# A hybrid decoder layer on one core: substitution's loads put ahead of its copies, heads' sums in two rounded passes, output projection's loads of rows and weights put amid tiles of x

## The chip, the core and the metric

The kernel runs on one core of one Trainium2 chip. The metric is device time in microseconds (us), the median of several runs; lower is better. Engines are named as the profile names them: PE multiplies matrices and transposes through a multiplication with the identity, PEld loads its weights, DVE and ACT work element by element, POOL does the small rest, and SP issues all DMAs of this kernel, in order, on one queue.

## The reference

One layer: a linear recurrence (RWKV-7) of 8 heads and forgetting attention of 8 heads share one input projection; their outputs share one output projection; a gated MLP with a short convolution follows. Everything is float32, 1024 tokens, 1024 channels.

```python
h = rmsnorm(x, norm_mix_w)
p = h @ w_in                                   # 1024 x 3848
y_rwkv = rwkv7_group(p[..., :1792], ...)       # state S: [64, 64] a head
y_fox  = fox_group(p[..., 1792:], ...)         # causal softmax with decay
x = x + concat([y_rwkv, y_fox]) @ w_out
h = rmsnorm(x, norm_ffn_w)
x = x + conv_glu_ffn(h, w_up, conv_w, conv_b, w_down)   # 2816 wide, twice
return rmsnorm(x, norm_final_w)

# in rwkv7_group, two sums over the 64 channels of a head:
kk = heads(k * k_k)
kk = kk * rsqrt(maximum(sum(kk * kk, axis=-1, keepdims=True), 1e-24))
bonus = sum(r_h * k_h * r_k, axis=-1, keepdims=True) * v_h
```

## The kernel before

**Precision.** A big product is made of three PE passes in the type `fp32r`: both operands are split into `hi` (a rounded copy, made by ACT as a CAST) and `lo` (the rest, source minus `hi`, made by DVE as a TENSOR_TENSOR), and `hi*hi + hi*lo + lo*hi` is added up in PSUM. Small products and transposes take plain float32 operands; the trace then holds two MATMUL records for a product of 512 columns.

**What sets the order.** No engine chooses its work at run time. The program is a set of generators ("streams"); each yields one instruction, or a list that must stay together, or a condition to wait for. A planner (`Streams`, line 56 on; all instructions are issued in its line 193, so every row of the profile says L193) keeps a time per engine from a cost table, takes the instruction that could start first, and breaks ties by `RANK` (line 35; the lower number goes first). The result is a fixed order for each engine. A moved rule therefore changes the order of nearly everything behind it.

**Stages, in the profile's names.**
- Input projection: `r` (14 column tiles of the recurrence, 672 matmuls with 512 columns) and then `t<-whi/wlo,hhi/hlo` (attention's columns, 1536 matmuls with 256 or 264 columns). Both are called *dense* below. They have PSUM banks and buffers of their own and fill PE wherever the other streams wait. `late` may start when all 2208 are done.
- Recurrence: names with `u_`, 8 *units* (4 pairs of heads, two halves of the tokens each), one stream for each step: `front` (decays; `ss` is the heads' sum of squares, `beta` comes from it), `gram`, `slots` (`bps` is the heads' sum for the bonus), `taken_out`, `inverse`, `placed`, `solve`, `chain` (the state's steps), `output`.
- The stream `inverse` inverts 32x32 triangles by substitution on POOL. `taken_out` writes the triangles to `dsub` in DRAM; `inverse` loads them four times, each time for 32 partitions of the tile `ml`, lets ACT copy a quarter of each into `mw`, runs 60 POOL instructions and stores `mw` to `dinv`; `placed` loads that into `tbd`, which `solve` needs.
- Attention (once all 8 units are out and the pools are handed over): `s` (scores), `t<-ident,pr` (transposes of the weights), `po` (products), `tt` (tails); `tq` turns queries and keys.
- Output projection, `op`: a first pass over 4 of 8 row tiles of `w_out` for all 8 token tiles (96 matmuls; allowed between attention's steps, since dense is then done), the sum put aside in `sp_x`, and a second pass for the rest (288). `plan` (line 1329) is the order in which the stream `late_loads` issues their loads and `late_splits` makes `hi` and `lo` of them: kinds `wo` (a tile of `w_out`), `y` (a row tile of the inputs that went to DRAM), `xh` (half a token tile of x, which the first pass adds to), `x`. The raw loads share four buffers (tag `f2`) with the input projection's evictions; the split weights share four `whi` and four `wlo` buffers, which come free when the last token tile has used them.
- MLP: `hT`, `A` to `F` (up), `dx` and `dy` (down).

The order of POOL's and SP's other work around the change comes from the same planner.

Of the kernel before, what the change touches and what calls it, by code (L numbers as in the profile page):

```python
# [32 lines left out]
INF = float("inf")  # L33

RANK = dict(rates=4, loads=2, params=4, fills=3, normed=4, turned=4, weights=3, splits=3, dense=9, evac=0, forget=8,
            chain=1, solve=2, inverse=7, taken_out=0, placed=6, front=3, gram=0, slots=4, output=5, stages=0, late_splits=8,
            late_loads=3, late=9, products=5, load_pairs=6, values=3, scores=0, soft=4, turned_back=2, tail=7,
            added=3, parts=1, summed=4, turned_again=4, combined=2, up_loads=6, sums=2.5, up_splits=2.5, down_loads=7,
            down_splits=2.5, token_loads=5, conv=9, combined_2=3,
# [235 lines left out]
def hymba_layer(tc, x, norm_mix_w, w_in, rwkv_mu, rwkv_w0, rwkv_w2, rwkv_a0, rwkv_a2, rwkv_g2, rwkv_k_k, rwkv_k_a,  # L275
# [8 lines left out]
    with whole:  # L284
# [5 lines left out]
        ident = cst.tile([P, P], F32, name="ident")  # L290
        make_identity(nc, ident)
        Q.given.update([ident.name] + [f"in_{n}" for n in _INS])
        oblk = cst.tile([P, P], F32, name="oblk")
        ones = cst.tile([P, P], F32, name="ones")
        mhalf = cst.tile([P, 16], F32, name="mhalf")
        prm = cst.tile([P, C_END], F32, name="prm")
        cvw = cst.tile([P, 3, 2 * NFF], F32, name="cvw")
        Q.do(V.memset(mhalf, -0.5), V.memset(oblk, 0.0), V.memset(oblk[0:64, 0:64], 1.0),
             V.memset(oblk[64:128, 64:128], 1.0), V.memset(ones, 1.0),)


        sp_r = {(j, p, h): dr.tile([P, HALF], F32, name=f"sp_{j}_{p}_{h}") for j in "rkv" for p in range(4)
# [441 lines left out]
        def names(i):  # L744
# [11 lines left out]

            return p, hf, u, tl, rp, col

        def front(i):
            p, hf, u, tl, rp, col = names(i)  # L760
            q = units[i]
# [9 lines left out]

            sq = tl("t2", "sq", [P, HALF], 6)
            yield S.activation(sq, kt_, AF.Square, scale=col(C_KK))
            pt = yield from rp("ss")
            yield PE.matmul(pt, lhsT=oblk, rhs=sq, start=True, stop=True)
            beta = tl("t2", "beta", [P, HALF], 6)
            yield V.tensor_scalar(beta, pt, scalar1=1e-24, scalar2=0.0, op0=ALU.max, op1=ALU.add)
            Q.release(pt)
# [79 lines left out]
        def slots(i):  # L858

            p, hf, u, tl, rp, col = names(i)  # L860
            q = units[i]
            yield has(i, "gram")
            kb = q["kb"]
            yield has(i - 2, "chain")
            kbt = tl("kbt", "kbt", [P, 8, P], 2)
            for nq in range(2):
                pt = yield from rp(f"kbt{nq}")
                for i4 in range(4):
                    n = nq * 4 + i4
                    m, o = divmod(n, 2)  # L870
                    yield PE.transpose(pt[:, i4 * P:(i4 + 1) * P],
                                       kb[:, m, 2 * o:2 * o + 2, :].rearrange("p a c -> p (a c)"), ident)
                yield S.copy(kbt[:, nq * 4:nq * 4 + 4, :].rearrange("p n c -> p (n c)"), pt)
                Q.release(pt)
            q["kbt"] = kbt
            yield lambda: ("r", 8 + p, hf) in done
            yield has(i - 2, "output")
            bv = tl("bv", "bv", [P, HALF], 2)
            yield SP.dma_start(bv, sp_r["v", p, hf])
            vu = tl("vu", "vu", [P, 8, P], 2)  # L880
            vu4 = vu.rearrange("p (m o) c -> p m o c", o=2)
            pt = yield from rp("vt")
            for m in range(4):
                yield PE.transpose(pt[:, m * P:(m + 1) * P], bv[:, m * P:(m + 1) * P], ident)
            yield S.copy(vu4[64:128, :, 0, :], pt[0:64].rearrange("p (m c) -> p m c", c=P))
            yield S.copy(vu4[0:64, :, 1, :], pt[64:128].rearrange("p (m c) -> p m c", c=P))
            Q.release(pt)
            q["vu"] = vu
            pt = yield from rp("bps")
            yield PE.matmul(pt, lhsT=oblk, rhs=q["rk"], start=True, stop=True)  # L890
            q["bonus"] = True
            yield V.tensor_tensor(bv, bv, pt, op=ALU.mult)
            Q.release(pt)
            q["bv"] = bv
# [14 lines left out]
        def inverse(i):  # L909
# [7 lines left out]
            ml = tl("ml", "ml", [P, 32, 32], 1)  # L917
            mw = tl("mw", "mw", [P, 8, 32], 1)
            tmp = tl("mtmp", "mtmp", [P, 72], 1)
            mwf = mw.rearrange("p a t -> p (a t)")  # L920
            for g in range(4):
                gs = slice(g * 32, g * 32 + 32)
                yield SP.dma_start(ml[gs], dsub.rearrange("q o b s t -> (q o b) s t"))
                yield S.copy(mw[gs], ml[gs, g::4, :])
            for s in range(1, 31):
                w, n = 31 - s, (s + 3) // 4
                tv = tmp[:, 0:n * w].rearrange("p (s t) -> p s t", t=w)
# [2 lines left out]
                yield G.tensor_tensor(mw[:, 0:n, s + 1:32], mw[:, 0:n, s + 1:32], tv, op=ALU.add)  # L930
            for g in range(4):
                yield G.memset(mwf[g * 32:g * 32 + 32, g::36], 1.0)
            for g in range(4):
                yield SP.dma_start(dinv.rearrange("q o b s t -> (q o b) s t")[:, g::4, :],
                                   mw[g * 32:g * 32 + 32])
            q["dinv"] = dinv

        def placed(i):
            q = units[i]
# [389 lines left out]
        def plan():  # L1329
            for kt in range(4):  # L1330
                yield "wo", (0, kt), w_out[0, kt * P:(kt + 1) * P, 0:HALF]
            for kt in range(7):
                for hf in (1, 0):
                    yield "y", (hf, kt), y_v[:, kt, half(hf)]
                if kt == 3:
                    for tb in TOKENS:
                        yield "xh", tb, x8[tb][:, 0:HALF]
            for j, k0, tbs in ((0, 4, ()), (1, 0, TOKENS[0:4]), (1, 4, TOKENS[4:])):
                for kt in range(k0, k0 + 4):
                    yield "wo", (j, kt), w_out[0, kt * P:(kt + 1) * P, half(j)]  # L1340
                for tb in tbs:
                    yield "x", (0, tb), sp_x[tb]
# [644 lines left out]
```

## Time and profile before

| | |
|---|---|
| time, median of 3 runs | 1462.68 us (1462.61 to 1465.28) |
| the profiled execution | 1458.29 us, its span 1456.5 us |
| busy in the span: PE, PEld, DVE, ACT, POOL | 1404.3, 1159.0, 1061.2, 712.8, 300.6 us |
| mean granted PE clock | 0.996 |
| 50 to 552.4 us: recurrence and dense | PE busy 492.47 of 502.40 us |
| 552.4 to 722.8 us: attention, rest of dense, first `op` | PE busy 158.11 of 170.40 us |
| 722.8 to 799.6 us: rest of `op` | PE busy 72.82 of 76.80 us |
| from 799.6 us: MLP | PE busy 644.71 of 656.90 us |

A matmul's duration in a row is longer than its share of PE, since matmuls overlap: what it costs is the step from its start to the next one's start. "Idle" is time with no matmul under way. Rows of the timeline give start, duration, engine, line, operation, `out<-in`, shapes, count, and in brackets the idle time before with what ended it.

### The profile page before, as it was taken

The page shows a single profiled execution, that of the slowest core. Times are in us where ns is not written, and L with a number is a line of the kernel's source. Part 1 is how long each engine was busy: PE and PEld are TensorE (multiplying, and loading weights), DVE is VectorE, ACT ScalarE, POOL GpSimd, SP SyncE. Part 2 cuts the span into 40 slices and gives each one's busy share as a digit, 9 for nine tenths or more (in the row PEclk, how much of TensorE's full clock was granted, in tenths as well). Part 3 has the DMA queues.
Part 4 walks back from the last instruction along what each step waited for, and adds up shares of the span by engine and source line. Part 5 has one row for each costly group of instructions (what it writes and reads, how often), then busy time and mean ns, then how long its engine had stood idle before and what let it go on. Part 6 is the DMA issues. An engine that isn't in the chain of part 4 may idle for free.

```text
span 1456.5 us, 23416 instructions
## 1 busy us (share of the span) xinstructions
PE 1404.3 (96%) x8105; PEld 1159.0 (80%) x8105; DVE 1061.2 (73%) x2036; ACT 712.8 (49%) x1339; POOL 300.6 (21%) x772
## 2 busy tenths in 40 slices
PE   6999999999999999989999989999999999999997
PEld 4777877889999998667678868888888888888886
DVE  5387567877775546787546898988887776896575
ACT  6643344445343336777533654455544544444453
POOL 3006553365465212433301000000000000000011
PEclk9999999999999999999999999999999999999999
DMA  5544333433422335474271134555652225864342
GB/s 178 195 120 136 97 95 111 123 102 100 113 68 78 87 104 154 136 213 132 90 267 65 62 113 156 190 188 195 202 167 80 73 86 187 305 199 139 95 152 87
DMA packets 198099, 198.12 MB, mean 136 GB/s; under 512 B 39979, under 2 KB 135773, under 8 KB 197981
## 3 DMA queue, kind: packets, MB, share of 16 engines
q1 hardware_dynamic: 197981, 196.63, 43.5%
q8 instruction: 64, 1.05, 0.3%
q14 instruction: 54, 0.44, 0.1%
HBM read 139.13 MB, written 57.44 MB: 135 GB/s over the span
## 4 chain that ended last, share of the span: by engine, by line
PE 77%; DVE 9%; DMA 6%; issue 3%; ACT 3%; SPq 1%; POOL 1%; DVEq 0%; POOLq 0%; ACTq 0%
PE B L193 16%; PE t L193 9%; PE r L193 8%; PE C L193 8%; PE dx L193 8%; PE dy L193 6%; PE op L193 4%; PE A L193 4%; PE u_uy L193 1%; DMA qraw<-sp_q 1%; PE s L193 1%; SPq L193 1%; PE po L193 1%; DMA x<-in_x 1%; DMA raw<-in_w_out 1%
## 5 line engine op out<-in xcount | busy, mean ns | idle before, releaser
L193 PE MATMUL t<-whi,hhi 128*128 128x256 f32 (+1 forms) x512 | 149.5, 292 | 1.2 <-ACT whi L193 0.8
L193 PE MATMUL t<-whi,hlo 128*128 128x256 f32 (+1 forms) x512 | 149.8, 293 | 0.0
L193 PE MATMUL t<-wlo,hhi 128*128 128x256 f32 (+1 forms) x512 | 149.1, 291 | 0.3 <-DVE wlo L193 0.3
L193 POOL TENSOR_SCALAR fms<-fms 128x1 f32<-128x1 f32 x8 | 2.4, 295 | 609.4 <-ACT fsq L193 609.1
L193 POOL TENSOR_TENSOR u_mtmp<-u_mw,u_ml 128x60 f32<-128x60 f32 (+10 forms) x240 | 79.1, 330 | 147.7 <-ACT u_mw L193 129.6
L193 ACT CAST dwhiP<-dP 128x512 fp32r<-128x512 f32 x77 | 47.7, 620 | 107.6 <-PE dy L193 48.4
L193 PEld LDWEIGHTS t<-whi,hhi 128*128 128x128 f32 x512 | 96.6, 189 | 3.6 <-ACT whi L193 1.0
L193 PEld LDWEIGHTS t<-wlo,hhi 128*128 128x128 f32 x512 | 96.6, 189 | 2.0 <-issue 1.0
L193 PEld LDWEIGHTS t<-whi,hlo 128*128 128x128 f32 x512 | 96.7, 189 | 1.9 <-issue 1.4
L193 PE MATMUL r<-hhi,whi 128*128 128x512 f32 x224 | 92.1, 411 | 0.9 <-DVE edge L193 0.6
L193 PE MATMUL r<-hlo,whi 128*128 128x512 f32 x224 | 92.7, 414 | 0.0
L193 PE MATMUL r<-hhi,wlo 128*128 128x512 f32 x224 | 91.7, 410 | 0.5 <-DVE wlo L193 0.5
L193 DVE TENSOR_TENSOR dwloP<-dP,dwhiP 128x512 fp32r<-128x512 f32 x77 | 53.1, 689 | 51.2 <-ACT dwhiP L193 50.8
L193 POOL TENSOR_TENSOR u_mw<-u_mw,u_mtmp 128x60 f32<-128x60 f32 (+10 forms) x240 | 83.9, 350 | 18.6
L193 DVE SCALAR_TENSOR_TENSOR yv<-uv,cvw,yv 128x1023 f32<-128x1023 f32 (+1 forms) x44 | 56.3, 1280 | 38.9 <-ACT yv L193 38.8
L193 PE MATMUL dx<-dwhiP,glP 128*128 128x512 f32 x176 | 69.4, 394 | 0.0
L193 PE MATMUL dx<-dwhiP,ghP 128*128 128x512 f32 x176 | 69.4, 394 | 0.0
L193 PE MATMUL dx<-dwloP,ghP 128*128 128x512 f32 x176 | 69.0, 392 | 0.0
L193 DVE SCALAR_TENSOR_TENSOR yg<-ug,cvw,yg 128x1023 f32<-128x1023 f32 (+1 forms) x44 | 56.4, 1282 | 7.6 <-ACT yg L193 6.7
L193 ACT CAST whi<-wraw 128x512 fp32r<-128x512 f32 (+1 forms) x60 | 37.0, 619 | 38.8 <-PE r L193 17.6
L193 ACT ACTIVATE pr<-pr,mx 128x1024 f32<-128x1024 f32 (+7 forms) x64 | 49.6, 779 | 9.3 <-DVE mx L193 9.1
L193 DVE TENSOR_TENSOR glP<-gb,ghP 128x512 fp32r<-128x512 f32 x77 | 52.7, 684 | 0.7 <-ACT ghP L193 0.6
(953 smaller groups left out, 4123.4 us busy)
## 6 DMA issues: line engine op xcount, KB each, us to landing
a<-in_ffn_w_up SPq DMA_DIRECT2D x88, 256.0 KB
wraw<-in_w_in SPq DMA_DIRECT2D x108, 128.0 KB
sp_gv<-yg SPq DMA_DIRECT2D x22, 512.0 KB
dB<-in_ffn_w_down SPq DMA_DIRECT2D x44, 256.0 KB
sp_T<-dB SPq DMA_DIRECT2D x44, 256.0 KB
gb<-sp_gv SPq DMA_DIRECT2D x44, 256.0 KB
dP<-sp_T SPq DMA_DIRECT2D x44, 256.0 KB
dP<-in_ffn_w_down SPq DMA_DIRECT2D x33, 256.0 KB
```

The costliest lines, as they stand in the source:

```text
L193: fn(*args, **kw)
```

## The change

It has three parts.

1. **Heads' sums.** `oblk` (the block matrix of ones) becomes `fp32r`, made from `ones`. `ss` and `bps` (8 of each) go through a new stream piece `head_sums`: ACT makes a rounded copy `hi`, DVE the rest `lo`, both in `f2` buffers, and PE adds two `fp32r` passes in one bank.
2. **Substitution.** `inverse` issues its four loads of `ml` first and its four copies to `mw` after them. The POOL part becomes a stream of its own, `substituted`, with the old rank 7; `inverse` itself (loads, copies, stores) and `placed` get rank 0.
3. **Output projection's loads.** `plan` puts all eight `y` items of the recurrence's rows first, then `xh` of four token tiles, then the `y` items of row tiles 4 and 5, `xh` of two, the `wo` tiles 4 and 5, `xh` of the last two, `y` of row tile 6, and `wo` 6 and 7. Before, all eight `xh` came ahead of `y` 4 to 6 and all four `wo`.

```diff
-RANK = dict(... solve=2, inverse=7, taken_out=0, placed=6, ...
+RANK = dict(... solve=2, inverse=0, taken_out=0, substituted=7, placed=0, ...
...
-        oblk = cst.tile([P, P], F32, name="oblk")
+        oblk = cst.tile([P, P], F32R, name="oblk")
...
+        def head_sums(name, src):
+
+            hi = yield from Q.take(fp, [P, HALF], F32R, "f2", f"{name}_hi", 4)
+            yield S.copy(hi, src)
+            lo = yield from Q.take(fp, [P, HALF], F32R, "f2", f"{name}_lo", 4)
+            yield V.tensor_tensor(lo, src, hi, op=ALU.subtract)
+            pt = yield from bank("rp", name, 3)
+            yield [PE.matmul(pt, lhsT=oblk, rhs=hi, start=True, stop=False),
+                   PE.matmul(pt, lhsT=oblk, rhs=lo, start=False, stop=True)]
+            Q.release(hi)
+            Q.release(lo)
+            return pt
...
-            pt = yield from rp("ss")
-            yield PE.matmul(pt, lhsT=oblk, rhs=sq, start=True, stop=True)
+            pt = yield from head_sums(f"{u}_ss", sq)
...
-            pt = yield from rp("bps")
-            yield PE.matmul(pt, lhsT=oblk, rhs=q["rk"], start=True, stop=True)
+            pt = yield from head_sums(f"{u}_bps", q["rk"])
...
+            quarters = [slice(g * 32, g * 32 + 32) for g in range(4)]
+            for gs in quarters:
+                yield SP.dma_start(ml[gs], dsub.rearrange("q o b s t -> (q o b) s t"))
+            for g, gs in enumerate(quarters):
+                yield S.copy(mw[gs], ml[gs, g::4, :])
+            Q.spawn("substituted", substituted(q, ml, mw, tmp))
+            yield has(i, "substituted")
...
-            for g in range(4):
-                gs = slice(g * 32, g * 32 + 32)
-                yield SP.dma_start(ml[gs], dsub.rearrange("q o b s t -> (q o b) s t"))
-                yield S.copy(mw[gs], ml[gs, g::4, :])
...
-            for kt in range(7):
+            def ys(kt):
                 for hf in (1, 0):
                     yield "y", (hf, kt), y_v[:, kt, half(hf)]
-                if kt == 3:
-                    for tb in TOKENS:
-                        yield "xh", tb, x8[tb][:, 0:HALF]
-            for j, k0, tbs in ((0, 4, ()), (1, 0, TOKENS[0:4]), (1, 4, TOKENS[4:])):
-                for kt in range(k0, k0 + 4):
+
+            def xhs_of(tbs):
+                for tb in tbs:
+                    yield "xh", tb, x8[tb][:, 0:HALF]
+
+
+            for kt in range(4):
+                yield from ys(kt)
+            yield from xhs_of(TOKENS[0:4])
+            yield from ys(4)
+            yield from ys(5)
+            yield from xhs_of(TOKENS[4:6])
+            for kt in (4, 5):
+                yield "wo", (0, kt), w_out[0, kt * P:(kt + 1) * P, 0:HALF]
+            yield from xhs_of(TOKENS[6:8])
+            yield from ys(6)
+            for j, k0, tbs in ((0, 6, ()), (1, 0, TOKENS[0:4]), (1, 4, TOKENS[4:])):
+                for kt in range(k0, (k0 + 4) & ~3):
```

**What stands where now.** In instructions, PE has 7241 instead of 7225, ACT 1254 instead of 1237, DVE 2053 instead of 2038, POOL 777 as before, SP 963 instead of 960 DMAs. From about the middle of the second `op` pass on, all five engines have the same order as before.

First place: SP, where unit 0's triangles go out to `dsub` and come back in `ml` (`sp_v`, `sp_k` and `sp_r` are rows of the projection that wait in DRAM, `u_bv`, `u_r`, `u_xs`, `u_k` and `u_ta` the units' loads of such rows, `wraw` weights of the input projection). Before:

```order
L193 DMA u_dsub<-u_ga 32x8x32 x4
L193 DMA u_bv<-sp_v_0_93 128x512
L193 DMA u_ml<-u_dsub 32x1024
L193 DMA sp_v_1_94<-pm_1_1149 128x512
L193 DMA u_ml<-u_dsub 32x1024
L193 DMA u_r<-sp_r_1_78 128x512
L193 DMA u_ml<-u_dsub 32x1024 x2
L193 DMA sp_k_0_87<-pm_0_1257 128x512
```

Now:

```order
L193 DMA sp_v_1_94<-pm_1_1109 128x512
L193 DMA u_dsub<-u_ga 32x8x32 x4
L193 DMA u_bv<-sp_v_0_93 128x512
L193 DMA u_ml<-u_dsub 32x1024 x4
L193 DMA sp_k_0_87<-pm_0_1208 128x512
L193 DMA wraw_2_1279<-in_w_in 128x2x128 x2
L193 DMA u_r<-sp_r_1_78 128x512
```

The four loads of `ml` follow each other; the load of `u_r`, which stood between them, now stands behind them and behind a load of weights.

Second place: SP, at the end of the first `op` pass (`raw<-in_x` is an `xh` load, `raw<-in_w_out` a tile of `w_out`, `sp_x` the stored sum of a token tile, `ot` a load of an attention tail). Before:

```order
L193 DMA raw_8764<-in_x 128x512
L193 DMA ot_8979<-sp_g_142 128x2x128
L193 DMA ot_9038<-sp_g_142 128x2x128
L193 DMA sp_x_145<-raw_8303 128x512
L193 DMA ot_9099<-sp_g_142 128x2x128
L193 DMA raw_9080<-sp_y 128x512
L193 DMA sp_x_146<-raw_8414 128x512
L193 DMA sp_x_147<-raw_8602 128x512
L193 DMA raw_9123<-in_w_out 128x512
L193 DMA raw_9154<-in_w_out 128x512
L193 DMA sp_x_148<-raw_8764 128x512
L193 DMA raw_9171<-in_w_out 128x512
```

Now:

```order
L193 DMA raw_9172<-in_x 128x512
L193 DMA raw_9198<-in_w_out 128x512
L193 DMA raw_9202<-in_w_out 128x512
L193 DMA sp_x_145<-raw_9095 128x512
L193 DMA sp_x_146<-raw_9172 128x512
L193 DMA raw_9211<-in_x 128x512
L193 DMA raw_9235<-in_x 128x512
L193 DMA raw_9251<-in_w_out 128x512
L193 DMA raw_9256<-in_w_out 128x512
L193 DMA raw_9261<-in_w_out 128x512
L193 DMA sp_x_147<-raw_9211 128x512
```

Two tiles of `w_out` now stand ahead of the stores `sp_x_145` and `sp_x_146` and of the last two `xh` loads; the other two stand behind these.

Third place: PE in attention. In PE's order before, 2093 of the 2208 dense matmuls stand ahead of the first scores, now 1982; of the first `op` pass, 93 matmuls stand ahead of attention's last tail before, 71 now. Between the scores' 61st and 73rd matmul PE's order before reads like this:

```order
L193 MATMUL t_7591<-ident,pr_7541 128x128 x4
L193 MATMUL tt<-ident,ot_7531 128x128 x2
L193 MATMUL t_7617<-ident,pr_7541 128x128 x3
L193 MATMUL s_0_7616<-k_7193,qhi_7400 128x512
L193 MATMUL s_0_7616<-k_7193,qlo_7401 128x512
L193 MATMUL t_7625<-ident,pr_7570 128x128 x4
L193 MATMUL s_512_7634<-k_7193,qhi_7400 128x256
L193 MATMUL s_512_7634<-k_7193,qlo_7401 128x256
```

and now like this:

```order
L193 MATMUL s_0_7619<-k_7170,qhi_7183 128x512
L193 MATMUL s_0_7619<-k_7170,qlo_7184 128x512
L193 MATMUL t_6_7520<-whi_2_6794,hlo 128x256
L193 MATMUL t_6_7520<-whi_2_6794,hhi 128x256
L193 MATMUL t_7628<-ident,pr_7542 128x128 x3
L193 MATMUL t_6_7520<-wlo_2_6795,hhi 128x256
L193 MATMUL t_6_7520<-whi_2_6794,hlo 128x256
L193 MATMUL t_6_7520<-whi_2_6794,hhi 128x256
L193 MATMUL tt<-ident,ot_7457 128x128
L193 MATMUL s_512_7646<-k_7170,qhi_7183 128x256
L193 MATMUL s_512_7646<-k_7170,qlo_7184 128x256
```

Dense matmuls (`t_6_7520<-whi`, `<-wlo`) now stand between scores and transposes where none stood.

More of the change, by code (lines that the diff above doesn't have):

```diff
@@ L35 @@
 RANK = dict(rates=4, loads=2, params=4, fills=3, normed=4, turned=4, weights=3, splits=3, dense=9, evac=0, forget=8,
-            chain=1, solve=2, inverse=7, taken_out=0, placed=6, front=3, gram=0, slots=4, output=5, stages=0, late_splits=8,
+            chain=1, solve=2, inverse=0, taken_out=0, substituted=7, placed=0, front=3, gram=0, slots=4, output=5, stages=0, late_splits=8,
             late_loads=3, late=9, products=5, load_pairs=6, values=3, scores=0, soft=4, turned_back=2, tail=7,
@@ L297, in hymba_layer @@
         cvw = cst.tile([P, 3, 2 * NFF], F32, name="cvw")
-        Q.do(V.memset(mhalf, -0.5), V.memset(oblk, 0.0), V.memset(oblk[0:64, 0:64], 1.0),
-             V.memset(oblk[64:128, 64:128], 1.0), V.memset(ones, 1.0),)
+        Q.do(V.memset(mhalf, -0.5), V.memset(ones, 1.0),
+             V.tensor_scalar(oblk, ones, scalar1=0.0, scalar2=0.0, op0=ALU.mult, op1=ALU.add),
+             V.tensor_copy(oblk[0:64, 0:64], ones[0:64, 0:64]), V.tensor_copy(oblk[64:128, 64:128], ones[64:128, 64:128]))
         sp_r = {(j, p, h): dr.tile([P, HALF], F32, name=f"sp_{j}_{p}_{h}") for j in "rkv" for p in range(4)
@@ L919, in inverse, with substituted @@
             tmp = tl("mtmp", "mtmp", [P, 72], 1)
+            quarters = [slice(g * 32, g * 32 + 32) for g in range(4)]
[5 more added lines that the diff above has]
+            yield has(i, "substituted")
+            for g in range(4):
+                yield SP.dma_start(dinv.rearrange("q o b s t -> (q o b) s t")[:, g::4, :],
+                                   mw[g * 32:g * 32 + 32])
+            q["dinv"] = dinv
+        def substituted(q, ml, mw, tmp):
             mwf = mw.rearrange("p a t -> p (a t)")
-            for g in range(4):
-                gs = slice(g * 32, g * 32 + 32)
-                yield SP.dma_start(ml[gs], dsub.rearrange("q o b s t -> (q o b) s t"))
-                yield S.copy(mw[gs], ml[gs, g::4, :])
             for s in range(1, 31):
@@ L932, in inverse @@
                 yield G.memset(mwf[g * 32:g * 32 + 32, g::36], 1.0)
[L933 to L936, printed above, removed]
+            q["substituted"] = True
         def placed(i):
```

## The prediction

> **What bounds the kernel now.** I read the page first, then busy time by stage, then PE's waits in each stage, then the timelines at the three places that the change touches.
>
> The page's part on busy time, and its slices, 36 us each:
>
> ```profile
> PE 1404.3 (96%) x8105; PEld 1159.0 (80%) x8105; DVE 1061.2 (73%) x2036; ACT 712.8 (49%) x1339; POOL 300.6 (21%) x772
> PE   6999999999999999989999989999999999999997
> ```
>
> PE is busy nearly everywhere. By stage (columns: stretch, length, then busy time of each engine with its instructions, granted clock, DMA share and rate):
>
> ```profile
> 50.00:552.40 502.40, 492.47 (x3716) 427.36 (x3716) 338.18 (x830) 208.10 (x415) 205.47 (x556) 1.00 0.39 109
> 552.40:722.80 170.40, 158.11 (x1088) 121.38 (x1089) 125.46 (x346) 119.59 (x291) 63.16 (x134) 0.99 0.47 138
> 722.80:799.60 76.80, 72.82 (x326) 57.24 (x325) 41.30 (x63) 27.05 (x55) 6.66 (x18) 1.00 0.50 169
> 799.60:1456.50 656.90, 644.71 (x2817) 525.45 (x2815) 526.92 (x741) 322.83 (x523) 14.15 (x30) 1.00 0.45 149
> ```
>
> Length minus PE's busy time: 9.9 us without a matmul in the recurrence's stage, 12.3 in attention, 4.0 in the output projection, 12.2 in the MLP, whose order the change leaves as it is. So there are two ways to gain: take work off PE (worth its full length in the first stage, where dense matmuls fill every wait), or close some of the 26 us of holes ahead of the MLP.
>
> **Part 1, heads' sums.** PE's timeline around unit 0's `bps` (start, duration):
>
> ```profile
> 102.59 0.39 PE L193 MATMUL r<-hhi,whi 128*128 128x512 f32 x1
> 102.83 0.39 PE L193 MATMUL r<-hhi,wlo 128*128 128x512 f32 x1
> 103.06 1.02 PE L193 MATMUL u_bps<-u_r,oblk 128*128 128x512 f32 x2
> 103.91 0.60 PE L193 MATMUL u_at<-ident,u_ar 128*128 128x128 f32 x4
> ```
>
> Starts count: an `fp32r` matmul of 512 columns takes 102.83 to 103.06, or 0.23 to 0.24 us; the float32 product takes 103.06 to 103.91, or 0.85. Two rounded passes cost 0.47, so 0.38 is saved. How many there are:
>
> ```profile
> L193 PE MATMUL u_ss<-u_sq,oblk x16: 592/592/697, 71.6 to 376.0; 128*128 128x512 f32 x16
> L193 PE MATMUL u_bps<-u_r,oblk x16: 590/592/697, 103.1 to 454.0; 128*128 128x512 f32 x16
> ```
>
> Two records a product, so 8 and 8, all inside the stage in which PE has 9.9 us of holes in 502. Saved: 16 x 0.38 = **6.1 us**. The new copies and differences are of the same kind and size as the split of a `w_out` tile (minimum, median, maximum in ns):
>
> ```profile
> L193 ACT CAST cwhi<-raw x4: 618/619/620, 725.5 to 729.7; 128x512 fp32r<-128x512 f32 x4
> L193 DVE TENSOR_TENSOR cwlo<-raw,cwhi x4: 691/693/693, 726.1 to 730.3; 128x512 fp32r<-128x512 f32 x4
> ```
>
> ACT gets 16 x 0.62 = 9.9 us on top of 208, DVE 16 x 0.69 = 11.1 on top of 338, in a stage of 502: DVE goes from 0.67 to 0.70 of it. What hides them is the dense work; a unit's `front` becomes 1.3 us longer from square to `beta`, 10.5 us over 8 units if nothing ran beside it. `bps` ends in `bv`, which is wanted only at a unit's output. The two `f2` buffers that a sum holds are of four that the dense evictions use too: if these come late, PE stands with both banks full. I price that at 0; its bounds are 0 and the wait below that is nearest to it (PE for `ACT whi`, 0.8 us once). Making `oblk` adds one DVE pass over 128 columns during the first loads: nothing.
>
> PE's waits in 100 to 552 us and in attention, the longest two of each (total, times, longest):
>
> ```profile
> PE u_ch L193 <- DVE u_vu L193: 2.7, 3, 1.3
> PE u_vt L193 <- DMA u_bv<-sp_v: 0.9, 1, 0.9
> ...
> PE t L193 <- ACT whi L193: 0.8, 1, 0.8
> ...
> PE s L193 <- DVE mx L193: 3.1, 5, 1.2
> PE t L193 <- ACT pt L193: 2.3, 7, 0.5
> ```
>
> **Part 2, substitution.** Unit 0's loads, last copy and first POOL step:
>
> ```profile
> 99.13 0.31 SPq L193 DMA_DIRECT2D u_ml<-u_dsub  x1
> 101.20 0.34 SPq L193 DMA_DIRECT2D sp_v<-pm  x1
> 101.58 0.43 SPq L193 DMA_DIRECT2D u_ml<-u_dsub  x1
> 104.11 0.34 SPq L193 DMA_DIRECT2D u_r<-sp_r  x1
> 104.49 0.90 SPq L193 DMA_DIRECT2D u_ml<-u_dsub  x2
> 109.15 0.40 ACT L193 COPY u_mw<-u_ml 32x256 f32<-32x256 f32 x1
> 109.63 0.24 POOL L193 TENSOR_TENSOR u_mtmp<-u_mw,u_ml 128x30 f32<-128x30 f32 x1 [81.14 <-ACT u_mw L193]
> ```
>
> From the first load to POOL 10.5 us pass. The two loads at 104.49 end their issue at 105.39, and POOL starts 4.2 us later. Issued together from 99.13, four loads of 0.45 us end at 100.9 and POOL could start at about 105: 4 to 5 us sooner a unit. SP carries the four ahead of one store and one load of `u_r` (0.34 us each); POOL's order within a unit is unchanged. On PE the gain is bounded by the waits that a late substitution can cause in this stage, a share of the 9.9 us; none of PE's waits there names `tbd`. So I count 0 directly. Bounds: 3.6 us gained (the waits for `u_vu` and `u_bv` above, 2.7 + 0.9), and 7.2 lost: `placed`, now at rank 0, makes SP wait for `dinv` with other loads queued behind it, and one wait as that for `u_bv`, 0.9 us, in each of 8 units is its price. I take the middle since neither has more than the quoted few waits to speak for it. What the part does is indirect: the units end earlier in PE's order, and 2093 - 1982 = 111 dense matmuls move into attention.
>
> **What that does to attention.** A dense matmul of 256 columns steps by 0.12 us:
>
> ```profile
> 525.82 0.28 PE L193 MATMUL t<-whi,hhi 128*128 128x256 f32 x1
> 525.94 0.28 PE L193 MATMUL t<-wlo,hhi 128*128 128x256 f32 x1
> ```
>
> 111 x 0.12 = 13.3 us of filling come in; 93 - 71 = 22 matmuls of `op` at 0.23 (5.1 us) leave towards the end. 8.2 us more filling meet 12.3 us of holes. Where it lies counts: between the 49th and the 97th score, where the order before has 2 dense and 5 `op` matmuls, there are now 55 dense; between the 97th and 133rd there are 3 `op` instead of 18. Waits like `s <- DVE mx` close in the first stretch and open in the second. I take **1.5 us** gained; bounds 8.2 gained (all filling falls into holes) and 3 lost (the 15 `op` matmuls missing, 3.5 us, all become holes and nothing closes).
>
> **Part 3, output projection's loads.** The end of the first `op` pass on PE, then SP:
>
> ```profile
> 723.37 0.40 PE L193 MATMUL op<-cwhi,hlo 128*128 128x512 f32 x1
> 726.15 0.50 PE L193 MATMUL op<-cwhi,hhi 128*128 128x512 f32 x1 [2.38 <-ACT cwhi L193]
> 726.88 0.50 PE L193 MATMUL op<-cwlo,hhi 128*128 128x512 f32 x1 [0.23 <-DVE cwlo L193]
> ...
> 728.60 0.50 PE L193 MATMUL op<-cwhi,hhi 128*128 128x512 f32 x1 [0.29 <-ACT cwhi L193]
> 729.33 0.50 PE L193 MATMUL op<-cwlo,hhi 128*128 128x512 f32 x1 [0.23 <-DVE cwlo L193]
> ...
> 730.34 0.50 PE L193 MATMUL op<-cwhi,hhi 128*128 128x512 f32 x1 [0.28 <-ACT cwhi L193]
> 731.07 0.50 PE L193 MATMUL op<-cwlo,hhi 128*128 128x512 f32 x1 [0.22 <-DVE cwlo L193]
> 718.50 3.33 SPq L193 DMA_DIRECT2D sp_x<-raw  x2
> 721.93 0.87 SPq L193 DMA_DIRECT2D raw<-in_w_out  x2
> ```
>
> The second pass's first tile is asked for at 721.93, behind stores on which SP waits 3.3 us, and its split ends three microseconds after PE is through: 3.63 us of holes, all but 0.4 of the stage's 4.0. Now `wo` 4 and 5 are loaded ahead of those stores. Their splits wait only for the `whi` buffers, which come free at the last token tile's 3rd and 6th matmul; 9 matmuls (2.1 us) are left then, against 0.62 + 0.69 for the split. `wo` 6 and 7 stand behind the stores of two token tiles and the last two `xh` loads. From the moment that PE ends the second of these two tiles it takes an add (0.69), a store (0.33), two loads and their own issue (0.45 each), 2.4 us as an estimate; then landing, from 721.93 to the end of the hole at 726.15 less a split's 0.62, some 3.6; then 0.62 + 0.69 for the split: 7.3. The work that PE has until then is 24 + 6 matmuls, 6.9 us. So up to half a microsecond may stay: **3.1 us** gained, bounds 3.6 gained and 0. Late next, where this goes, is the MLP's start, whose order is as before. Two more rows of `y` go through DRAM with one more load and split (0.62 and 0.69, ACT and DVE are 0.7 busy in attention): 0.
>
> **The sum.** 6.1 + 0 + 1.5 + 3.1 = 10.7 us, off the profiled execution's 1458.3: 1447.6. That execution lies 4.4 us under the median 1462.68 of the runs; against the median it gives **1452.0 us**. No change can be told from one under 0.2% (2.9 us).
>
> **The rivals.**
> - *Only the arithmetic.* The stall comes back at `wo` 6 or at attention's second half: 1462.7 - 6.1 = 1456.6. For it: SP waits in order, and 6.9 against 7.3 is close. Against: even half the stall gone shows.
> - *All the filling falls into holes.* 6.1 + 3.1 + 8.2 = 17.4 gained: 1445.3. Against: the later stretch has less filling than before.
> - *POOL and DVE in each other's way.* Beside a DVE instruction with two SBUF inputs a POOL step of 28 columns takes twice as long as one of 52 columns a little later:
>
> ```profile
> 112.06 0.57 POOL L193 TENSOR_TENSOR u_mtmp<-u_mw,u_ml 128x28 f32<-128x28 f32 x1
> 114.79 0.28 POOL L193 TENSOR_TENSOR u_mtmp<-u_mw,u_ml 128x52 f32<-128x52 f32 x1
> 112.45 0.72 DVE L193 TENSOR_TENSOR u_ar<-u_ar,u_beta 128x512 f32<-128x512 f32 x1
> ```
>
>   Sixteen new differences with two SBUF inputs, each holding POOL for its whole 0.69, would be 11.1 us on the substitution; if that set the end, 10.7 gained and 11.1 lost, 1463.1, no change. Against: PE names no wait for `tbd`, and 4 us a unit come back from the loads. The Trainium skill (SBUF — State Buffer, Who interferes with whom) says that a DVE instruction with two SBUF inputs contends with a GpSimd one that reads SBUF, and that whichever starts second blocks fully. The rows above agree with the contention; by the row the price is 0.3 us for each, 4.8 in all, 1456.8.
> - *The cover is gone (slower).* The units' steps stand closer in PE's order, with 111 dense matmuls fewer among them. If the state's chain (`u_ch <- DVE u_vu`) cannot run that close, PE waits bare by up to those 13.3 us, and the total is 1452.0 + 13.3 = 1465.3. It decides once holes in the first stage grow by 10.7 us, from 9.9 to over 20. Against: there they are 2% now, under orders made by the same rules.
>
> **How the numbers follow.** Forecast 0.55 (own range 1449 to 1455.5), only the arithmetic 0.20, all filling used 0.10, POOL and DVE 0.06, cover gone 0.09. Faster by over 0.2%: 0.85; within: 0.06; slower: 0.09. The range 1446.0 to 1459.5 holds the forecast, the arithmetic and half of the third, 0.80.
>
> **What would show it.** Right: `u_ss` and `u_bps` as 32 records stepping by 0.23; the first scores near 533 us (552.4 - 13.3 - 6.1); no wait of PE for `cwhi` over 0.5 us; four loads of `ml` in a row and POOL some 6 us behind the first. Wrong: holes over 15 us ahead of the first scores, waits of PE for `s` or `tt` beyond 12 us in attention, or a new wait on `cwhi` at `wo` 6. The MLP should last 656.9 us as before.

## The result, and the profile after

| | before | changed |
|---|---|---|
| median of 10 runs each on one chip (us) | 1463.22 (1461.69 to 1465.28) | 1454.73 (1451.50 to 1461.85) |
| ratio, 95% interval | | 0.9947 [0.9932, 0.9961] |
| a second time, with the experiments (us) | 1463.06, 23 runs | 1455.36, 6 runs, ratio 0.9951 [0.9936, 0.9967] |
| mean granted clock of all runs | 0.9922 (57 runs) | 0.9934 (16 runs) |

The kernel is 7.7 to 8.5 us faster; the forecast was 10.7 us (1452.0). The first profiled execution of the changed kernel took 1461.85 us, 7 over its median, so the profile read here is that of its second run, `after_again`, 1453.13 us with a span of 1451.4.

Busy time of the page, then the four stages of that profile, cut at the first score, the end of attention and the first matmul of the MLP (columns as in the prediction):

```profile
PE 1399.1 (96%) x8105; PEld 1162.8 (80%) x8105; DVE 1071.3 (74%) x2051; ACT 719.9 (50%) x1356; POOL 298.5 (21%) x772
50.00:533.80 483.80, 474.13 (x3601) 415.25 (x3600) 344.58 (x839) 211.70 (x425) 201.00 (x554) 1.00 0.40 110
533.80:713.20 179.40, 165.52 (x1176) 131.57 (x1177) 127.37 (x350) 123.15 (x299) 65.50 (x135) 0.99 0.49 139
713.20:794.00 80.80, 78.36 (x349) 62.84 (x348) 42.59 (x65) 27.25 (x56) 6.64 (x18) 0.98 0.50 168
794.00:1451.40 657.40, 645.71 (x2817) 526.08 (x2815) 527.12 (x741) 322.76 (x522) 14.15 (x30) 1.00 0.45 149
```

The recurrence's stage is 18.6 us shorter, attention 9.0 longer, the output projection 4.0 longer and the MLP 0.5 longer. Without a matmul are 9.7 us in the first stage (9.9 before), 13.9 in attention (12.3), 2.4 in the output projection (4.0). So almost no waiting went away; what went is work: PE's busy time fell by 5.2 us. PE's two longest sums of waits in attention (total, times, longest):

```profile
PE s L193 <- ACT qhi L193: 3.2, 2, 2.7
PE s L193 <- DVE mx L193: 3.1, 5, 1.1
```

**Part 1.** A pair of passes for unit 0 and the row behind it, then all pairs of `ss` (records, minimum, median and maximum in ns, first and last start):

```profile
71.80 0.40 PE L193 MATMUL u_ss<-u_ss_hi,oblk 128*128 128x512 f32 x1
72.03 0.39 PE L193 MATMUL u_ss<-u_ss_lo,oblk 128*128 128x512 f32 x1
72.27 0.40 PE L193 MATMUL r<-hhi,whi 128*128 128x512 f32 x1
...
L193 PE MATMUL u_ss<-u_ss_hi,oblk x8: 390/435/498, 71.8 to 376.6; 128*128 128x512 f32 x8
L193 PE MATMUL u_ss<-u_ss_lo,oblk x8: 388/394/403, 72.0 to 376.8; 128*128 128x512 f32 x8
```

From 71.80 to 72.27 is 0.47 us, as forecast, where the float32 product took 0.85.

**Part 2.** Unit 0's four loads, the last two copies and POOL's first step:

```profile
99.29 1.71 SPq L193 DMA_DIRECT2D u_ml<-u_dsub  x4
...
104.45 0.82 ACT L193 COPY u_mw<-u_ml 32x256 f32<-32x256 f32 x2
105.35 0.24 POOL L193 TENSOR_TENSOR u_mtmp<-u_mw,u_ml 128x30 f32<-128x30 f32 x1 [77.26 <-ACT u_mw L193]
```

POOL starts 6.1 us behind the first load; it was 10.5. Over the eight units the same distance is 4.7 to 7.1 us, together 47 against 85. A unit ends with its product with the gate, so the last of the eight tells where the recurrence is through (`u_gps`, kernel before and changed kernel):

```profile
L193 PE MATMUL u_gps<-u_sg,g x16: 590/592/597, 200.7 to 536.4; 128*128 128x512 f32 x16
```

```profile
L193 PE MATMUL u_gps<-u_sg,g x16: 590/592/595, 191.2 to 518.2; 128*128 128x512 f32 x16
```

**Part 3.** SP at the end of attention, then PE behind the last token tile of the first `op` pass:

```profile
711.73 3.58 SPq L193 DMA_DIRECT2D sp_x<-raw  x2
715.40 1.93 SPq L193 DMA_DIRECT2D raw<-in_x  x2
718.62 1.49 SPq L193 DMA_DIRECT2D raw<-in_w_out  x3
...
718.89 0.40 PE L193 MATMUL op<-cwhi,hlo 128*128 128x512 f32 x1
720.02 0.47 PE L193 MATMUL op<-cwhi,hhi 128*128 128x512 f32 x1 [0.73 <-DVE raw L193]
723.05 0.50 PE L193 MATMUL op<-cwhi,hhi 128*128 128x512 f32 x1 [1.40 <-ACT cwhi L193]
723.78 0.50 PE L193 MATMUL op<-cwlo,hhi 128*128 128x512 f32 x1 [0.22 <-DVE cwlo L193]
```

The wait of 2.38 us for `wo` 4 is gone, and PE waits at `wo` 6 instead, whose load again stands behind two stores of `sp_x`.

**The clock.** PE's busy time and the granted clock in neighbouring stretches of 3.4 us (stretch, length, busy time of PE with its matmuls, clock, then DMA share and rate) around three waits of the changed kernel:

```profile
584.70:588.10 3.40, 0.90 (x6) 1.00 0.66 176
588.10:591.50 3.40, 3.40 (x17) 0.50 0.25 78
591.50:594.90 3.40, 3.40 (x26) 1.00 0.31 83
721.20:724.60 3.40, 1.78 (x6) 1.00 0.86 277
724.60:728.00 3.40, 3.40 (x9) 0.51 0.73 219
833.90:837.30 3.40, 0.79 (x3) 1.00 0.00 0
837.30:840.70 3.40, 3.14 (x6) 0.50 0.00 0
```

Behind each stretch with little work comes one at half the clock. The span of an execution times its mean clock is called its time *at full clock* below, and the rest of the span is what it *lost to half clock*. This charges each microsecond at half clock half a microsecond, which is the full price; how much of it the runs show is worked out under the table.

### The profile page after: what moved, and what is told of

The parts are those of the page before. It is cut to its first block, busy times and chain, and to the rows that moved or that the text cites. A ratio compares the mean times of both kernels' runs of the same rounds, so it can differ in the third digit from the quotient of the medians.

```text
span 1460.1 us, 23486 instructions
## 1 busy us (share of the span) xinstructions
PE 1405.5 (96%) x8105; PEld 1167.7 (80%) x8105; DVE 1070.8 (73%) x2051; ACT 720.3 (49%) x1356; POOL 297.7 (20%) x772
## 4 chain that ended last, share of the span: by engine, by line
PE 65%; DVE 4%; DMA 3%; issue 2%; ACT 2%; POOL 1%; SPq 0%; DVEq 0%; POOLq 0%; ACTq 0%
PE B L193 16%; PE t L193 9%; PE C L193 8%; PE dx L193 8%; PE dy L193 6%; PE op L193 5%; PE A L193 4%; PE s L193 2%; DMA qraw<-sp_q 2%; PE po L193 1%; PE u_uy L193 1%; PE D L193 1%; DMA raw<-in_w_out 1%; PE hT L193 0%; DMA x<-sp_x 0%
## 5 line engine op out<-in xcount | busy, mean ns | idle before, releaser
L193 POOL TENSOR_TENSOR u_mtmp<-u_mw,u_ml 128x60 f32<-128x60 f32 (+10 forms) x240 | 75.0, 312 | 135.4 <-ACT u_mw L193 110.1
L193 POOL TENSOR_TENSOR u_mw<-u_mw,u_mtmp 128x60 f32<-128x60 f32 (+10 forms) x240 | 84.2, 351 | 18.5
L193 DVE TENSOR_TENSOR wlo<-wraw,whi 128x512 fp32r<-128x512 f32 (+1 forms) x60 | 41.4, 691 | 19.7 <-ACT whi L193 18.9
L193 ACT CAST whi<-wraw 128x512 fp32r<-128x512 f32 (+1 forms) x60 | 37.0, 619 | 37.4 <-PE t L193 17.9
```

The source lines that it names most:

```text
L193: fn(*args, **kw)
```

## The experiments

The theory that the first comparison left (A): the gain is PE's arithmetic alone; what the new order wins at one wait it loses at another; and the time that executions lose to half clock differs with the waits. The rival (B): the gain comes from the moved loads, as the prediction's terms for attention and part 3 have it.

**The changed kernel again, for a typical profile.**

> The changed kernel once more, for a profile of an execution near its median. Theory A (the gain is PE work saved and idle PE time closed ahead of the MLP; the profiled execution of the changed kernel was long because TensorE's clock fell to half for three stretches of 6.8 us behind PE's waits): ratio 0.993 to 0.996 as before, 1453 to 1456 us in the median; in this profile fewer stretches at half clock than three, the time shorter by about 3.4 us for each one missing, and attention's idle time near 14 us. Theory B (the gain comes from the output projection's loads): the same ratio, and the idle time of PE between the last token tile of the first pass and the MLP under 1 us instead of 4.

1455.36 us, three stretches of half clock of 3.41 us each between 50 and 1440 us, where the first profile of the same kernel had three of 6.83. Half of the 10.2 us that this is more makes 5.1 of the 8.7 us between the two spans. PE's waits between the first pass and the MLP come to 2.4 us, not under 1. So B fails; A holds but for the number of stretches, which are as many and each half as long, and it leaves 3.6 us between the two spans, of which a stretch at 37 us in the first profile alone can make 1.7.

**A table of two arithmetics by two orders.** In `arith_frozen` the kernel before gets two passes over one rounded tile:

```diff
-            sq = tl("t2", "sq", [P, HALF], 6)
+            sq = tl("t2", "sq", [P, HALF], 6).bitcast(F32R)
...
-            yield PE.matmul(pt, lhsT=oblk, rhs=sq, start=True, stop=True)
+            yield [PE.matmul(pt, lhsT=oblk, rhs=sq, start=True, stop=False),
+                   PE.matmul(pt, lhsT=oblk, rhs=sq, start=False, stop=True)]
...
```

`bps` is changed in the same way, and `oblk` holds blocks of 0.5.

> The kernel before with the arithmetic of the heads' sums alone: the square and r*k are written rounded by the instructions that make them, and the same tile is multiplied twice by blocks of one half in fp32r (no second, low half: that leaves the rounding error of the sums in). No copy, no difference, no f2 buffer is added, and the order of all engines is that of the kernel before, instruction by instruction. Theory A (in this stage every wait is filled, so PE work counts in full): 16 x 0.38 = 6.1 us less, 1456.6 against 1462.7, ratio 0.9958. Theory B (the stage is set by the chain of units, and PE's saving turns into idle time): ratio above 0.999 and 10 to 16 us of idle PE time between 50 us and the first scores instead of 9.9.

In `order_f32` the changed kernel gets the float32 product back, with everything else in its place (`hi` becomes a float32 copy and `lo` the maximum of source and copy, so that ACT and DVE have the same work):

```diff
-            yield [PE.matmul(pt, lhsT=oblk, rhs=hi, start=True, stop=False),
-                   PE.matmul(pt, lhsT=oblk, rhs=lo, start=False, stop=True)]
+            yield PE.matmul(pt, lhsT=oblk, rhs=lo, start=True, stop=True)
```

> The order of the changed kernel, instruction by instruction on all engines, with the arithmetic of the kernel before: in place of the rounded value and the difference two float32 copies are made by the same two engines, and one float32 product over them stands where the two rounded passes stood. With the kernel before, arith_frozen and the changed kernel this fills a table of two orders by two arithmetics. Theory A (arithmetic and order add up; the new order leaves less half clock, 9.5 us of work lost against 12): span times granted clock 1449 to 1450 us, and 2 to 3 us faster than the kernel before, 1459 to 1461, ratio 0.998 to 0.9985. Theory B (the order is worth nothing by itself): ratio 1.000. Theory C (the prediction's terms for the order, 1.5 + 3.1): ratio 0.9969.

| | order before | order after |
|---|---|---|
| float32 product: median | 1462.3 (57 runs) | 1460.4 (12 runs), ratio 0.9993 [0.9982, 1.0003] |
| at full clock / lost to half clock | 1449.1 / 11.4 | 1449.2 / 9.4 |
| two rounded passes: median | 1458.5 (12 runs), ratio 0.9974 [0.9963, 0.9985] | 1454.7 (16 runs) |
| at full clock / lost to half clock | 1443.7 / 13.4 | 1443.9 / 9.6 |

(Means of span times clock; their standard errors are 0.3 to 0.8 us, those of the losses 0.3 to 0.7. About 2 us of each loss lie behind PE's last matmul, where every profile has half clock and it costs nothing.) At full clock the arithmetic is worth 5.4 and 5.3 us and the order nothing. The order leaves 2.1 and 3.7 us less half clock, with errors of about 0.8.

In time itself the picture is less clean. The means are 1462.3 and 1460.3 us in the upper row, 1458.8 and 1455.2 in the lower one: the arithmetic is worth 3.4 us in the order before and 5.1 in the order after, and the order 1.9 and 3.6, with errors of 0.6 to 0.9. How much of the order's part is half clock hangs on the price, and the full price is too high. Among the 143 executions of these comparisons, each set against the mean of its own group, one microsecond more of loss goes with 0.57 us more of span (error 0.06). At that price the arithmetic is worth 4.5 and 5.2 us, and the order, apart from half clock, 0.7 and 1.4, each less than twice its error. So the arithmetic carries half to three quarters of the 7.0 us between the kernels, and of the order's part more than half is half clock. `order_f32` alone isn't told from the kernel before, the interval reaches from 0.18% faster to 0.03% slower. The profile of `arith_frozen` has five stretches of half clock ahead of the MLP's end, one of them 10.24 us long.

**Part 3 undone** (`p12`: `plan()` as in the kernel before):

> The changed kernel with part 3 undone: the output projection's loads stand as in the kernel before. Prediction's step: part 3 is worth 3.1 us, so this is 3 us slower than the changed kernel, ratio to the kernel before 0.9965 against 0.9945. What the profile of the changed kernel says (the wait went from one of 2.4 us at the second pass's first tile to three of 0.7 to 1.5 us at wo 6 and at the second half's first tile): equal to the changed kernel within 1 us, with one wait of 2 to 3 us for cwhi near 725 us again.

1455.06 us, ratio 0.9944 [0.9928, 0.9960] against 0.9951 of the changed kernel beside it; 1443.9 at full clock, as with part 3. Its profile has the one wait back:

```profile
721.54 0.40 PE L193 MATMUL op<-cwhi,hlo 128*128 128x512 f32 x1
724.92 0.79 PE L193 MATMUL op<-cwhi,hhi 128*128 128x512 f32 x1 [2.98 <-ACT cwhi L193]
725.64 0.79 PE L193 MATMUL op<-cwlo,hhi 128*128 128x512 f32 x1
```

With two of 0.2 us behind it, PE's waits in this stage come to 3.4 us, against 2.4 with part 3. In time no difference is found: the medians lie 0.3 us apart, with errors of about 1 us.

**Part 2 undone** (`p13`: substitution's loop, its one stream and its ranks as in the kernel before):

> The changed kernel with part 2 undone: each quarter's load stands before its copy again, and the ranks are those before. In its order all 2208 dense matmuls stand ahead of the first scores (1982 in the changed kernel, 2093 before): a unit's front is longer by the two copies and differences, so the units end later. Theory A (the heads' sums need part 2: without it the longer front takes the filling out of attention): first scores near 562 us, more idle PE time in attention than 20 us, 3 to 9 us slower than the changed kernel, 1458 to 1464. Theory B (part 2 does nothing, as the prediction's direct term of 0 has it): equal to the changed kernel within 1.5 us.

1481.91 us, ratio 1.0125 [1.0103, 1.0147]: slower than the kernel before by 1.25%, and than the changed kernel by 26.6 us, three times the upper end of what A expected. Its first stage and attention, PE at their boundary, and the last `u_gps`:

```profile
50.00:581.10 531.10, 508.04 (x3856) 446.18 (x3855) 361.26 (x865) 225.21 (x449) 213.82 (x562) 0.99 0.39 109
581.10:770.50 189.40, 169.83 (x1051) 124.78 (x1052) 128.90 (x350) 122.06 (x297) 56.48 (x133) 0.98 0.52 156
...
566.66 0.63 PE L193 MATMUL tq<-ident,qkt 128*128 128x128 f32 x4 [2.86 <-DVE qkt L193]
576.19 0.79 PE L193 MATMUL op<-cwhi,hhi 128*128 128x512 f32 x1 [8.90 <-ACT hhi L193]
581.12 0.77 PE L193 MATMUL s<-k,qhi 128*128 128x512 f32 x1 [1.73 <-ACT qhi L193]
...
L193 PE MATMUL u_gps<-u_sg,g x16: 590/592/595, 208.4 to 563.2; 128*128 128x512 f32 x16
```

The last unit ends at 563, 45 us later than in the changed kernel. All 2208 dense matmuls are used up before that, PE stands still for 15 us between 560 and 581, and attention has no dense matmul left to fill its waits: 19.6 us of holes. Half clock takes its share, at the full price 19.2 us on average against 9.6. POOL starts 8.4 to 18.5 us behind a unit's first load here, 101 us over eight units. The run undoes the place of the loads and the ranks together, and the planner makes a new order of it; which of these the 26.6 us hang on, it does not show.

**Part 1 undone** (`p23`: `oblk` in float32 and one product for each sum; the loads stay moved):

> The changed kernel with part 1 undone: the heads' sums are one float32 product each again, substitution's loads and the output projection's loads stay moved. 1909 dense matmuls ahead of the first scores. Theory A (the gain is the arithmetic alone; the moved filling is worth nothing): 6 us slower than the changed kernel, 1460 to 1462, span times granted clock near the 1449.5 us of the kernel before (1443.3 to 1444.2 in the changed one). Theory B (the prediction's other terms, 1.5 + 3.1): 1458.

1463.04 us, ratio 1.0002 [0.9990, 1.0015], and 1449.0 at full clock, within 0.1 us of the kernel before. Parts 2 and 3 without part 1 do nothing to the time, although the first score comes at 531.7 instead of 552.4. That is A, a little beyond its range; half clock takes 11.9 us here.

**The queries' loads ahead of a broadcast.** The wait ahead of 588 us is for `qhi`, whose load stands behind that of `nb`, 512 KB; `q_first` swaps them (and lets the scores wait for `nb` too):

```diff
+                    yield from queries(p, 1, h)
                     nb = yield from Q.take(bp, [P, T], F32, "nb", f"nb{p}{h}", 3)
                     yield SP.dma_start(nb, sp_c[2 * p + h:2 * p + h + 1, :].partition_broadcast(P))
                     d["nb", h] = nb
-                    yield from queries(p, 1, h)
```

> The changed kernel with the loads of a head's second half of queries ahead of the broadcast load of its nb row instead of behind it (and six buffers instead of five for the rows' sums, which the moved order needs). Theory A (the waits of 2.0 to 2.6 us for qhi in attention come of the queries' loads landing 6.3 us after their issue behind the broadcast, and the half clock follows these waits): no wait of PE for qhi over 1 us, attention's idle time under 11 us instead of 14.5, no stretch of half clock in attention, 3 to 7 us faster than the changed kernel. Theory B (the loads land late because of all transfers then, wherever they stand): the wait for qhi stays at 2 us, or a wait of the same length for mx behind the late nb row takes its place; no gain within 1 us.

1462.09 us, ratio 1.0002 [0.9991, 1.0014]: 7 us slower than the changed kernel, and 1450.1 at full clock against 1443.9. PE's waits in its attention (total, times, longest), then two of ACT's casts of queries:

```profile
PE s L193 <- DVE mx L193: 6.6, 12, 1.3
...
PE tt L193 <- ACT ot L193: 2.4, 1, 2.4
...
PE po L193 <- ACT ot L193: 2.0, 1, 2.0
...
529.41 0.62 ACT L193 CAST qhi<-qraw 128x512 fp32r<-128x512 f32 x1 [2.38 <-DMA qraw<-sp_q]
...
591.23 0.62 ACT L193 CAST qhi<-qraw 128x512 fp32r<-128x512 f32 x1 [2.02 <-DMA qraw<-sp_q]
```

No wait of PE for `qhi` is left. The casts that waited for their loads show what the place does: the loads of the first of these, ahead of a broadcast, were there 2.7 us after the second was issued (526.7), those of the other, right behind one, after 6.9 us (584.3); in the changed kernel it was 6.4 us (580.1 to 586.53). But PE's waits for `mx` have doubled from 3.1 us, two of 2 us for `ot` are new, attention has 17.9 us of holes, and half clock takes 11.1. The edit also moved the order of attention as a whole. So the first half of A, that the loads land late because of their place, is borne out; as a gain it failed.

**PE's waits filled.** In `filled` small matmuls stand at three places, each ahead of the matmul that waits:

```diff
+                for _ in range(n):
+                    if fresh:
+                        nc.tensor.matmul(args[0][:, 0:P], lhsT=oblk, rhs=oblk, start=True, stop=True)
...
```

With `fresh` the matmul behind them overwrites what they leave; in the other branch they add zeros.

> The changed kernel, the order on all engines the same, with small matmuls put into four of PE's waits that came back in its profiles: 20 of 128 columns ahead of the score that waits 2.1 to 3.7 us for qhi near 590 us, 5 and 11 ahead of the output projection's two waits for cwhi near 723 us, 17 and 4 ahead of the MLP's two waits of 2.0 and 0.6 us for T near 840 us. Their results are overwritten, or they add zeros. At about 0.11 us each they take the time that PE stands still there, so they cost nothing if the wait is as long. Theory A (the half clock follows idle PE time): no stretch at half clock near 590, 724 and 840 us, each of which was there in two or three of three profiles of this order (3.4 or 6.8 us long); 10 to 17 us of half clock less, 4 to 7 us faster than the changed kernel, 1448 to 1451 us. Theory B (it is not idle time, or 2 us more do not count): the stretches stay, the time is the changed kernel's or up to 2 us longer.

1453.65 us, ratio 0.9945 [0.9925, 0.9965]. Its profile, at the same places as above:

```profile
584.24 2.43 PE L327 MATMUL s<-oblk 128*128 128x128 f32 x20
586.50 0.45 PE L331 MATMUL s<-k,qhi 128*128 128x512 f32 x1
...
584.60:588.00 3.40, 3.40 (x30) 2.81 (x30) 0.69 (x1) 1.97 (x4) 0.19 (x1) 1.00 0.92 230
588.00:591.40 3.40, 3.40 (x23) 3.00 (x23) 2.90 (x8) 2.20 (x5) 0.00 (x0) 1.00 0.15 45
724.40:727.80 3.40, 3.17 (x14) 2.55 (x14) 0.91 (x2) 0.86 (x2) 0.00 (x0) 1.00 0.86 183
836.80:840.20 3.40, 1.99 (x7) 0.76 (x6) 3.40 (x6) 1.99 (x3) 0.00 (x0) 1.00 0.00 0
...
620.80:624.20 3.40, 1.70 (x10) 1.06 (x9) 2.25 (x5) 3.40 (x10) 1.91 (x2) 1.00 0.63 228
624.20:627.60 3.40, 3.19 (x13) 1.99 (x15) 2.85 (x12) 1.41 (x6) 0.17 (x2) 0.51 0.77 233
```

The clock stays full at all three places, and drops at a fourth that was not filled, and once ahead of 50 us. The time expected of it did not come: over its six runs the clock is 0.9938, and the median lies 1 to 2 us under the changed kernel's, within the error.

**More waits filled** (`filled_more`):

> The changed kernel, order the same, with small matmuls in nine more of PE's waits than the kernel filled had: at 36 us (z, 10 and 5), at the first score (9), in four more waits of attention (9, 9, 4 and 4), and in three more of the MLP's waits for T. filled had no half clock at its three places in its profile, yet its executions averaged a granted clock of 0.9938 like the changed kernel's. Theory A (half clock follows idle PE time, and goes on to the next wait of a microsecond where one is filled): with all of these filled the mean granted clock is 0.9955 or higher, the profile has at most one stretch of half clock before the end, and the time is 2 to 4 us under the changed kernel's, 1451 to 1453. Theory B (it falls at random): mean clock 0.993 to 0.9945 as before, time 1454 to 1456.

Mean clock 0.9946, just above what B expected, and one stretch of half clock ahead of the end, 6.83 us from 620.0. The stretch ahead of it has 1.8 us without a matmul, in waits for `qkt` and `ot` that this run does not fill either. 7.9 us are lost to half clock instead of 9.6, but at full clock the kernel takes 1446.6 us instead of 1443.9, with an error of 1.0. The likely reason is filling that is longer than its wait; no run shows it place by place. 1455.41 us, no gain.

**The kernel before again:**

> The kernel before once more, for a second profile: its first one ran at a granted clock of 0.996, above the 0.992 that its other executions average. Theory A (stretches of half clock behind PE's waits make executions differ): more half clock than 6.8 us between 50 and 1450 us, behind the same waits at 598, 633, 726 or 842 us, and a span longer than 1456.5 by half of what is more. Theory B (executions differ for other reasons): the same two stretches and a longer span.

1460.67 us, clock 0.992: four stretches of half clock between 50 and 1440 us, 17.1 us in all against 3.4 in the first profile. Three stand behind the waits at 601, 728 and 844 us that A names, one at 315 us that it doesn't, and none at 633. The span is 2.5 us longer; half of the 13.7 us more would be 6.8. So A is right on what happens and not on its full price. That part of a slower stretch falls into waits that are there anyway would explain this; it isn't shown.

**What half clock follows.** All 12 profiles have half clock in pieces of 3.41 us or a multiple, and those of one execution lie on one grid. (The last piece is cut short by the end.) Laid over the traces, that grid gives 4933 windows at full clock from 24 us on. Of 41 windows in which PE was idle for 1.6 us or more, 36 were followed by half clock; of 12 with 1.4 to 1.6 us, 3; of 4880 with less, 2. So half a window of idle time is about the limit in these traces, and a wait of 2 us can count or not by how it falls on the grid. It isn't the whole rule: five windows with more stayed without effect. In the first profile of the kernel before, one at the MLP's first waits had 1.44 us of work in 3.40, and the clock stayed:

```profile
838.30:841.70 3.40, 1.44 (x7) 0.86 (x5) 3.15 (x6) 0.62 (x1) 0.00 (x0) 1.00 0.18 53
841.70:845.10 3.40, 2.20 (x6) 0.97 (x6) 3.40 (x6) 1.61 (x3) 0.00 (x0) 1.00 0.00 0
```

This is a count over profiles, and the filling is its one trial, at three places; how the clock fell in the executions without a profile is known from their means alone. The Trainium skill (TensorE: Matmul & The Clock Gate, Part 1: The HAM clock gate) gives a free-running window of 3413 ns, which these traces bear out. It has the clock halved after an idle window of about that length; here windows with work in them were enough, 1.78 us from 721.20 and 1.70 us from 620.80 in the rows above.

## Why the prediction was right or wrong

- *Part 1, 6.1 us.* Right in mechanism and about right in size: 5.4 and 5.3 us at the full price of half clock, 4.5 and 5.2 at the lower one, with errors of about 0.8. That ACT's and DVE's 21 us of added work stay hidden holds only with part 2 beside it (`p13`). The price of 0 for them was right for the change as a whole and not for its first part.
- *Part 2, direct 0.* Right as a sum, for the kernel with the old arithmetic (`p23`). The step that failed is that the parts were priced one by one. POOL's start came 4.4 us sooner in unit 0, as worked out, and 38 us sooner over eight units. The kernel before has no use for this; with the heads' copies and differences in place, part 2 is worth 26.6 us. That a unit's longer front makes the difference is argued: without part 2 the last unit ends 27 us later than in the kernel before (563.2 against 536.4).
- *Attention, 1.5 us.* Wrong in mechanism: the holes did not close, they are 13.9 us against 12.3 (12.9 in the second profile before). The order as a whole is worth 1.9 and 3.6 us in time, but more than half of that is less half clock, and what is left, 0.7 and 1.4 us, is less than twice its error. The waits for `mx` sum to 3.1 us as before, and those for `qhi` grew from 0.4 to 3.2 us, behind loads that landed 6.4 us after their issue. Filling that enters a stage does not meet its holes by itself.
- *Part 3, 3.1 us.* Wrong: no gain within the error of about 1 us. The step that failed is the path of `wo` 6, which the prediction led from PE's second token tile over an add, a store and two loads. SP had issued these two loads by 717.33, and then waited for something that is in no term, the split of `wo` 4 (ACT and DVE, then SP's waits between 716 and 720 us in total, times, longest):

```profile
717.24 1.31 ACT L193 CAST cwhi<-raw 128x512 fp32r<-128x512 f32 x2 [3.34 <-PE op L193]
717.89 1.38 DVE L193 TENSOR_TENSOR cwlo<-raw,cwhi 128x512 fp32r<-128x512 f32 x2 [2.95 <-ACT cwhi L193]
...
SPq L193 <- DVE cwlo L193: 1.5, 2, 1.2
```

  `wo` 6 needs a raw buffer, and one came free when `wo` 4 was split, at 718.59; that split had itself waited for the `whi` buffers of the last token tile. So SP asks for `wo` 6 at 718.62, 0.3 us ahead of the first pass's last matmul (718.89). From there its split began 3.8 us later, near the 3.6 us of the prediction. The wait that was to stay at up to half a microsecond was 1.40 + 0.22, with 0.73 for the add of a token tile ahead of it. The sign "a new wait on `cwhi` at `wo` 6" came true.
- *The clock* is in no term. The loss fell from 11.4 to 9.6 us, errors 0.3 and 0.6. At the full price this brings 5.2 to 7.0, which is what the means of all runs differ by (1462.3 and 1455.2); at the price of 0.57 it is 1.0 us.
- *The rivals.* "Only the arithmetic" (1456.6, chance 0.20) has the mechanism that the runs bear out: the stall came back at `wo` 6. "Cover gone" did not come, but `p13` shows a wait of its kind: there the dense matmuls are used up before the last unit ends, instead of standing in attention, and the first stage's holes grow to 23.1 us. "POOL and DVE" left no trace: POOL's busy time fell from 300.6 to 298.5 us. Of its rows, the POOL step at 112.06 ran for the most part beside another DVE difference, that of a weight tile from 111.81, and not beside the one shown.
- *What would show it.* The pairs at 0.23 apart, the first score at 533.8 (near 533), the four loads in a row with POOL 6.1 us behind, and the MLP at 657.4 us were right; "no wait of PE for `cwhi` over 0.5 us" was not. So the range and the sign held for the reason given first. That the central value was only 2.7 us low is luck in part: the two terms for waits, 4.6 us, stand on holes that would close, and ahead of the MLP these are 26.0 us against 26.2. What the new order gave in their place is for more than half less half clock, which is in no term.

## What to carry to other kernels

Here, where PE is busy 96% of the time and an order fills its waits, PE's work taken off counted nearly in full, and moved waits left the sum of the holes as it was. Before pricing a wait away, follow the load that is late next back to every buffer and store that it waits for. Price two edits that share a path together as well as singly: the one that is worth nothing alone can be what the other needs. When the clock of executions differs, compare span times clock as well as the time, and check from executions of one program what half clock really costs; here the same arithmetic showed as 3.4 us in one order and 5.1 in the other.

## What was not expected of the hardware

By its mean clock an execution loses 9 to 13 us to half clock at the full price, and about 0.57 of that by its time. The stretches follow waits of no more than 2 to 3 us: 1.6 us of idle time within one window of 3.41 us were followed by one 36 times in 41. Which waits count differs from one execution to the next. The changed kernel's times lie 10 us apart (1451.50 to 1461.85), but the clocks of these two executions, 0.993 and 0.991, account for 3 us of that at most; the rest stays open. Small matmuls of 128 columns, twenty in 2.4 us, went with a full clock at the places where they filled the wait, but the executions were no faster on average.
